# A Hymba decoder layer on one core: where the gates of the second in-projection stand, and which pages the first steps of the second out-projection use

## The chip, the cores and the metric

One Trainium2 chip, one of its cores. The metric is the device time of one execution in microseconds (us); of several runs the median is taken. TensorE (PE) multiplies; VectorE (DVE), ScalarE (ACT) and GpSimd (POOL) work element by element; SP issues most of the DMAs, POOL some of them.

## The reference

A single layer (depth 1) over 2048 positions of width 1024, all in float32, and a last RMSNorm. Without its input generator:

```python
h = rms_norm(x, norm1_g)
z = einsum('bsd,de->bse', h, w_in)              # 1024 -> 3584
lru_x, lru_gate, sc_b, sc_c, sc_x = split(z)    # 1024, 1024, 512, 512, 512
lru_x = causal_dwconv(lru_x, lru_conv_w) + lru_conv_b        # 4 taps
r = sigmoid(lru_x @ wa + ba); i = sigmoid(lru_x @ wx + bx)   # 16 heads of 64
a = exp(-8 r softplus(-lambda)); b = sqrt(1 - a^2) * i * lru_x
h_t = a_t h_(t-1) + b_t                                      # scan over positions
y_lru = h * gelu(lru_gate)
y_sc = sc_b * causal_dwconv(sc_c * sc_x, sc_conv_w)          # 3 taps
x = x + concat(y_lru, y_sc) @ w_out                          # 1536 -> 1024
h = rms_norm(x, norm2_g)
u = causal_dwconv(h @ w_up, ffn_conv_w)                      # 1024 -> 6144, 3 taps
x = x + (gelu(gate) * up) @ w_down                           # 3072 -> 1024
out = rms_norm(x, final_g)
```

## The kernel before, in words

**Halves and stages.** The positions are worked in two halves of 1024. In order of time: the first half's in-projection (`in_phase(0)`, to about 335 us), its out-projection (`sweeps(0, .., "o")`, to 455 us), the second half's in-projection (`in_blocks`, to 753 us), its out-projection (`sweeps(1, .., "o")`, to 886 us), then `up_phase(0)`, `sweeps(0, .., "d")`, `up_phase(1)` and `sweeps(1, .., "d")`, the feed-forward network of each half. Features lie on the 128 partitions, positions along the free axis.

**A product in three.** An operand in float32 is written as hi + lo by `split` (L229): ACT copies it to the faster matmul type (hi, L230), DVE subtracts that copy from it (lo, L231). A product is then hi by hi, hi by lo and lo by hi. So each weight or activation page that PE reads has first cost one ACT and one DVE instruction, 128x1024 or 128x512.

**Seven products for eight.** Most projections use a Strassen-like scheme: of a matrix and an operand cut in 2x2 blocks, seven block products are formed of blocks and of sums of blocks. A product in `in_blocks` is 4 k-slices of 3 matmuls 128x128 by 128x512, 12 matmuls.

**The second in-projection.** `in_blocks` goes through 14 pairs of output blocks: L0 B0 L1 X0 L2 X1 L3 L4 L5 B2 L6 X2 L7 X3. An L pair holds the LRU input and the LRU gate of 128 channels; B and X pairs belong to the short convolution. A loop turn j issues the first products of pair j between the last ones of pair j-1: first (W11), second (W12) of pair j, seventh (W22) of pair j-1, the gates, fourth (S2) of pair j, sixth (S4) of pair j-1, third (S1) and fifth (S3) of pair j. When pair j-1 is done, `finish` issues the convolution of its LRU input (`conv`, L345 on ACT and three taps L347 on DVE, into a page named cv), and in the next turn come its gates: `lru_gates` (8 small matmuls, L371) and `lru_scan`: eight sigmoids of 64x512 on ACT (L382), then, with table loads between them, exp, tanh, square, square root and gelu on ACT (L387 to L398) and on DVE L385, L390, L392, the scan over positions L395 and the product L400. The outputs are combined for the out-projection's seven operands by DVE (L553 to L560) and stored to DRAM by POOL (L217).

Each product's partial result is copied from PSUM by ACT (L679) or added by DVE (L683); a matmul into the same bank must wait for its copy.

**The second out-projection.** `sweeps` makes 7 sweeps of 3 steps, one sweep for each of the seven products; a step multiplies two k-slices of weight by two of activation for four row blocks, 24 matmuls (L995). For a step SP loads a weight page and an activation page raw (L1008), and `split` makes of them four pages: wh, wl, fh, fl. The activation pages are what POOL stored in the stage before. Step 3, the first of sweep 1, reads the operand T1, which the last two units end.

**Pages.** SBUF has a few rotating pools: 28 pages "act" (`act`; in `in_blocks` they hold the normed input of the half, and come free as the last pairs use it), 10 pages for split weights and for `in_blocks`' cv, r and output pages (`wpage`, `vpage`: whoever asks next gets the page that has been out longest), 6 raw pages, 7 temporaries, 2 + 2 big ones. Steps below `lead` put their four split pages in act pages, with priority LW; the others in wpages with priority HW:

```python
with tc.high_priority(offset=LW if step < lead else HW):
    ...
    home = act if step < lead or ... else wpage
```

**What sets the order.** PE, SP and POOL issue in program order. DVE and ACT are ordered by the compiler's scheduler, from dependencies and the priorities given by `high_priority`; once set, each engine runs its list in that order. So a change of program text on PE also moves DVE and ACT rows.

**Beside the sweeps.** During the second out-projection, `h_beside(0, ...)` prepares the up-projection's four operands of the first half (`h_prep`: two loads ha and hb, DVE L609 to L616, and four splits), one at each of the four named steps. `up_phase` starts with the split weights of its first two pairs (`up_weights`), a `spread` that does pair 0 k by k, and 23 further pairs. Before everything, PE runs `WARM` matmuls of ones (L1043), until the first operands are there.

Of the kernel before, what the change touches and what calls it, by code (L numbers as in the profile page):

```python
# [28 lines left out]
NR = 6  # L29
LP = 0  # L30
LW = 400
NS = 2
J0 = 2
LEAD = 3
HALVES = (slice(0, P // 2), slice(P // 2, P))
HW = 90
HE = 30
WARM = 9
NOUT = NLRU + NSC
NI = NFF // 2  # L40
NO = NOUT // 2
# [49 lines left out]
def block_kernel(  # L91
# [59 lines left out]
    def wpage(name):  # L151
        turn[0] += 1
        return wv_page(name, "w" if turn[0] * NW % NWV < NW else "v")
# [10 lines left out]
    def raw_tile(name):  # L164
        return page(name, "wr", NR)
# [462 lines left out]
    def up_weights(half, j):  # L628
        n = f"up{half}_{j}"
        ta, tb, tcd = (raw_tile(f"wr{k}_{n}") for k in "abc")  # L630
        nc.sync.dma_start(ta[:, 0, :], w_up[j, 0])
        nc.sync.dma_start(tcd, w_up[j, 2:4].rearrange("h p c -> p h c"))
        nc.sync.dma_start(tb[:, 0, :], w_up[j, 1])
        tick()

        def two(src, name):
            hi, lo = wpage(f"wh{name}_{n}"), wpage(f"wl{name}_{n}")
            split(hi, lo, src)
            return [(hi[:, i, :], lo[:, i, :]) for i in range(2)]

        def add(dst, a, b):
            nc.vector.tensor_tensor(dst, a, b, ALU.add)

        w11, w12, w22, w21 = ta[:, 0, :], tb[:, 0, :], tcd[:, 0, :], tcd[:, 1, :]
        s1, s2, s3, s4 = ta[:, 1, :], tb[:, 1, :], tcd[:, 1, :], ta[:, 1, :]
        add(s1, w22, w21)
        add(s2, s1, w11)
        add(s3, w11, w21)
        p11, p1 = two(ta, "a")
        p12, p2 = two(tb, "b")  # L650
        p22, p3 = two(tcd, "c")
        add(s4, s2, w12)
        d = wpage(f"whd_{n}")
        split(d[:, 0, :], d[:, 1, :], s4)
        return {"W11": p11, "W12": p12, "W22": p22, "S1": p1, "S2": p2, "S3": p3, "S4": (d[:, 0, :], d[:, 1, :])}
# [124 lines left out]
            combine_odd(f_d[half], when, j // 2, a, cu, c, (cg[:, :NB], cg[:, NB:]))  # L780

    def up_phase(half, hs, between):
        wts = [up_weights(half, 0), up_weights(half, 1)]
        cur = UpPair(half, 0, hs, wts[0])
        for j in range(NFF):
            if j + 2 < NFF:
                wts.append(up_weights(half, j + 2))
            nxt = UpPair(half, j + 1, hs, wts[j + 1]) if j + 1 < NFF else None
            if j == 0:
                cur.spread()  # L790
                nxt.begin()
                nxt.sum1()
            elif nxt is None:
                cur.middle(cur.sum1)
                cur.second()
                cur.fourth()
                cur.end()
            else:
                cur.middle(cur.second)
                nxt.begin()  # L800
                cur.fourth()
                if j + 2 < NFF:
                    nxt.sum1()
                cur.end()
            up_rest(half, j, cur.ug, cur.un)
            cur = nxt
            between(j)
# [76 lines left out]
    def in_blocks(hs, start):  # L884
        half = 1
        gates = {}
        gain = {}
        wts = [{} for _ in PAIRS]
# [46 lines left out]
        open_gates = []  # L935
        for j in range(count + 1):
            tick()
            load(*uses(j + 1), rest=j + 1 >= count)
            if j == 0:
                pairs[0].spread()  # L940
                finish(pairs[0])
                start(0)
                continue
            cur = pairs[j] if j < count else None
            prev = pairs[j - 1] if j > 1 else None
            if cur:
                cur.first_term()
                cur.second_term()
            if prev:
                prev.seventh_term()  # L950
            for name in open_gates:
                gated, scanned = gates.pop(name)
                scanned(gated())
            open_gates = []
            if cur:
                cur.fourth_term()
            if prev:
                prev.sixth_term()
                finish(prev)
            open_gates = list(gates)  # L960
            if cur:
                cur.third_term()
                cur.fifth_term()
            if j < count:
                start(j)
# [10 lines left out]
    def sweeps(half, wsrc, fsrc, ni, name, residual, done, beside, tail=0, lead=0):  # L976
# [6 lines left out]
        for s, (wo, fo, on_x) in enumerate(SWEEPS):  # L983
# [20 lines left out]
            for i2 in range(ni // 2):  # L1004
# [5 lines left out]
                parts = []  # L1010
                with tc.high_priority(offset=LW if step < lead else HW):
                    for raw, n in zip(raws, "wf"):
# [28 lines left out]
    warm = pst("warm")  # L1041
    for i in range(WARM):
        nc.tensor.matmul(warm[:, :P], ones, ones, start=True, stop=True)  # L1043
# [124 lines left out]
    def h_beside(half, at):  # L1168
        def beside(s):
            if s in at:  # L1170
                hs[half].append(h_prep(half, len(hs[half]), rs2[half][0]))

        return beside

    prepare = h_beside(0, (4, 8, 12, 17))

    def out1_beside(s):
        if s == 0:
# [13 lines left out]
        out1_beside,  # L1192
        lead=LEAD,
    )
# [4 lines left out]
    def beside_pairs(j):  # L1199
        mean1(j)  # L1200
        for _ in range(NS if j >= J0 else 0):
            sum_step()
# [156 lines left out]
```

## Time and profile before

| What | Value |
|---|---|
| median of 3 runs | 2275.21 us (2275.09 to 2276.2) |
| the profiled execution | 2275.72 us, its span 2273.9 us |
| PE busy | 2228.6 us, 98% of the span |
| DVE, ACT, POOL busy | 1788.1, 1214.4, 173.8 us |
| mean granted TensorE clock | 0.993 |

Times below are microseconds from the span's start. A row of the timeline gives the start, the duration, the engine, the line, the operation with its output and inputs, the shape, and in brackets the time for which the engine stood idle ahead of it and what it then waited for. PE's duration of one matmul (0.39 us) overlaps the next one's: from start to start it is 0.227 us at the full clock, so that 12 matmuls take 2.72 us. A row of the windows view gives, for a stretch, the busy time of each engine with its instructions, the granted clock as a share of the full one, the share of DMA time and the rate.

### The profile page before, as it was taken

The page shows a single profiled execution, that of the slowest core. Times are in us where ns is not written, and L with a number is a line of the kernel's source. Part 1 is how long each engine was busy: PE and PEld are TensorE (multiplying, and loading weights), DVE is VectorE, ACT ScalarE, POOL GpSimd, SP SyncE. Part 2 cuts the span into 40 slices and gives each one's busy share as a digit, 9 for nine tenths or more (in the row PEclk, how much of TensorE's full clock was granted, in tenths as well). Part 3 has the DMA queues.
Part 4 walks back from the last instruction along what each step waited for, and adds up shares of the span by engine and source line. Part 5 has one row for each costly group of instructions (what it writes and reads, how often), then busy time and mean ns, then how long its engine had stood idle before and what let it go on. Part 6 is the DMA issues. An engine that isn't in the chain of part 4 may idle for free.

```text
span 2273.9 us, 26402 instructions
## 1 busy us (share of the span) xinstructions
PE 2228.6 (98%) x9750; PEld 1819.8 (80%) x9750; DVE 1788.1 (79%) x2070; ACT 1214.4 (53%) x1403; POOL 173.8 (8%) x298
## 2 busy tenths in 40 slices
PE   9999999999989799999999999999999999999997
PEld 7787787888768588888888888888888888888886
DVE  8868878947777898898888887676988888876556
ACT  7648834457797544455554444454544444443343
POOL 0021110000000100012111100000000000000000
PEclk9999999999999899999999999999999999999999
DMA  7585367833533865488782357674233232359764
GB/s 280 158 235 173 111 235 246 296 112 130 172 116 110 288 242 205 149 219 252 206 203 99 117 188 284 216 258 152 84 103 116 91 118 88 118 189 347 245 196 155
DMA packets 157952, 415.00 MB, mean 183 GB/s; under 512 B 16640, under 2 KB 19328, under 8 KB 157248
## 3 DMA queue, kind: packets, MB, share of 16 engines
q1 hardware_dynamic: 136960, 356.96, 45.7%
q0 software_dynamic: 20720, 56.37, 9.5%
q8 instruction: 76, 1.25, 0.2%
q14 instruction: 52, 0.43, 0.1%
q10 hardware_dynamic: 144, 0.00, 0.0%
HBM read 311.55 MB, written 139.46 MB: 198 GB/s over the span
## 4 chain that ended last, share of the span: by engine, by line
PE 86%; DVE 5%; ACT 4%; issue 3%; DMA 1%; POOL 0%; DVEq 0%; SPq 0%; ACTq 0%; POOLq 0%
PE zx L668 22%; PE dx L995 11%; PE zc L668 11%; PE zin_b L286 10%; PE dy L995 9%; PE za L668 6%; PE ox L995 5%; PE oy L995 4%; PE zxin L668 3%; PE zcin L668 1%; PE zS L668 1%; PE zain L668 1%; PE zr_b L371 1%; PE zW L668 1%; DVE r L395 1%
## 5 line engine op out<-in xcount | busy, mean ns | idle before, releaser
L231 DVE TENSOR_TENSOR fl_d<-wrf_d,fh_d 128x1024 fp32r<-128x1024 f32 x84 | 102.6, 1223 | 121.4 <-ACT fh_d L230 119.0
L230 ACT ACTIVATE fh_d<-wrf_d 128x1024 fp32r<-128x1024 f32 x84 | 88.9, 1059 | 202.4 <-PE dy L995 77.8
L995 PE MATMUL dx<-fh_d,wl_d 128*128 128x512 f32 x384 | 149.4, 389 | 0.0
L995 PE MATMUL dx<-fl_d,wh_d 128*128 128x512 f32 x384 | 149.4, 389 | 0.0
L995 PE MATMUL dx<-fh_d,wh_d 128*128 128x512 f32 x384 | 149.4, 389 | 0.0
L286 PE MATMUL zin_b<-xh,wl_in 128*128 128x512 f32 x448 | 138.2, 389 | 2.6 <-DVE wl_in L231 2.6
L286 PE MATMUL zin_b<-xh,wh_in 128*128 128x512 f32 x448 | 139.3, 392 | 0.9 <-ACT wh_in L230 0.8
L286 PE MATMUL zin_b<-xl,wh_in 128*128 128x512 f32 x448 | 138.3, 390 | 0.1
L231 DVE TENSOR_TENSOR wla_up<-wra_up,wha_up 128x1024 fp32r<-128x1024 f32 x48 | 58.8, 1225 | 101.0 <-ACT wha_up L230 101.0
L347 DVE SCALAR_TENSOR_TENSOR cg<-ug,prm,cg 128x1024 f32<-128x1024 f32 x96 | 122.9, 1280 | 9.5 <-ACT cg L343 8.5
L347 DVE SCALAR_TENSOR_TENSOR cu<-un,prm,cu 128x1024 f32<-128x1024 f32 x96 | 122.7, 1278 | 4.6 <-ACT cu L343 4.3
L668 PE MATMUL zc<-hhB,whd_up 128*128 128x512 f32 x368 | 120.8, 389 | 0.0
L668 PE MATMUL zx<-ht,whc_up 128*128 128x512 f32 x368 | 113.3, 389 | 0.0
L995 PE MATMUL dy<-fh_d,wh_d 128*128 128x512 f32 x288 | 112.1, 389 | 0.0
L995 PE MATMUL dy<-fl_d,wh_d 128*128 128x512 f32 x288 | 112.1, 389 | 0.0
L995 PE MATMUL dy<-fh_d,wl_d 128*128 128x512 f32 x288 | 112.1, 389 | 0.0
L231 DVE TENSOR_TENSOR wl_d<-wrw_d,wh_d 128x1024 fp32r<-128x1024 f32 x84 | 102.2, 1218 | 8.6 <-ACT wh_d L230 7.2
L679 ACT ACTIVATE ug<-zx 128x512 f32<-128x512 f32 x92 | 54.8, 595 | 101.2 <-PE zx L668 96.4
L230 ACT ACTIVATE fh_o<-wrf_o 128x1024 fp32r<-128x1024 f32 x42 | 44.5, 1059 | 111.5 <-PE ox L995 36.7
L286 PEld LDWEIGHTS zin_b<-xh,wh_in 128*128 128x128 f32 x448 | 83.5, 188 | 24.4 <-DVE xl L422 3.0
L286 PEld LDWEIGHTS zin_b<-xh,wl_in 128*128 128x128 f32 x448 | 84.0, 188 | 20.4 <-DVE wl_in L231 3.0
L286 PEld LDWEIGHTS zin_b<-xl,wh_in 128*128 128x128 f32 x448 | 84.1, 188 | 18.0 <-DVE xl L455 0.6
(549 smaller groups left out, 6394.6 us busy)
## 6 DMA issues: line engine op xcount, KB each, us to landing
wrc_up<-in_w_up SPq DMA_DIRECT2D x48, 512.0 KB, 4.9
f_d_T<-cg SPq DMA_DIRECT2D x96, 256.0 KB, 2.5
wrw_d<-sd_d_S SPq DMA_DIRECT2D x48, 512.0 KB, 5.1
wrf_d<-f_d_T SPq DMA_DIRECT2D x48, 512.0 KB, 4.3
f_d_B<-cu SPq DMA_DIRECT2D x72, 256.0 KB, 2.5
wrw_d<-in_w_down SPq DMA_DIRECT2D x36, 512.0 KB, 4.8
wrf_d<-f_d_B SPq DMA_DIRECT2D x36, 512.0 KB, 3.3
wr_in<-in_w_in SPq DMA_DIRECT2D x25, 512.0 KB, 7.1
```

What stands on the lines that cost most here:

```text
L230: nc.scalar.activation(r32(hi), src, AF.Copy)
L231: nc.vector.tensor_tensor(r32(lo), src, hi, ALU.subtract)
L286: nc.tensor.matmul(ps[t], r32(a), r32(b[:, blk(t)]), start=(first and i == 0), stop=(last and i == 2))
L347: nc.vector.scalar_tensor_tensor(dst, src[:, k : k + T], col(o_w + k), dst, ALU.mult, ALU.add)
L371: nc.tensor.matmul(ps[t], gw[rows, :], cv[rows, blk(t)], start=True, stop=True)
L395: nc.vector.tensor_tensor_scan(h, a, i, init, ALU.mult, ALU.add)
L668: nc.tensor.matmul(ps, r32(p[:, s]), r32(self.hs[k][x][o]), start=f and i == 0, stop=l and i == 2, skip_group_check=True,)
L679: nc.scalar.activation(dst, self.x, AF.Copy)
L995: nc.tensor.matmul(ps[m], r32(p), r32(x[:, k, :]), start=first and i == 0 and n == 0, stop=(last or not on_x) and i == ni - 1 and n == 2, ...
```

## The change

There are five edits. The gates of an open L pair come, on PE, after the fourth product of pair j and not ahead of it (GP = 1; in the last turn, where there is no pair j, nothing moves). Five leading steps of the second out-projection and not three use act pages and priority LW. In both up phases, the first pair's `up_weights` is under a priority of its own (UPP), which the scheduler of DVE and ACT sees. There are eleven warm-up matmuls and not nine. And the four operands of the first up phase are prepared at steps 4, 10, 15 and 19 and not at 4, 8, 12 and 17.

```diff
-LEAD = 3
+LEAD = 5
+GP = 1
+UPP = 200
-WARM = 9
+WARM = 11
     def up_phase(half, hs, between):
-        wts = [up_weights(half, 0), up_weights(half, 1)]
+        with tc.high_priority(offset=UPP):
+            wts = [up_weights(half, 0)]
+        wts.append(up_weights(half, 1))
...
             if prev:
                 prev.seventh_term()
-            for name in open_gates:
-                gated, scanned = gates.pop(name)
-                scanned(gated())
-            open_gates = []
-            if cur:
-                cur.fourth_term()
+            for p in range(3):
+                if p == GP:
+                    for name in open_gates:
+                        gated, scanned = gates.pop(name)
+                        scanned(gated())
+                    open_gates = []
+                if p == 0 and cur:
+                    cur.fourth_term()
+                if p == 1 and prev:
+                    prev.sixth_term()
             if prev:
-                prev.sixth_term()
                 finish(prev)
...
-    prepare = h_beside(0, (4, 8, 12, 17))
+    prepare = h_beside(0, (4, 10, 15, 19))
```

The line numbers of the changed kernel are 2 higher than those before, 4 higher behind `up_phase`, 7 higher behind `in_blocks`. On PE and POOL nothing else moves; on SP the loads of the second to fourth of the operands move with their steps. DVE's and ACT's lists change from the second in-projection on.

The first place is DVE in turn 9 of `in_blocks`, ahead of the gates of L4 (cv_4 is the page that these gates read; r_3, i_3 belong to L3's scan; wS, wW are weights of pairs 9 and 10). Before:

```order
L390 SCALAR_TENSOR_TENSOR cv_3_4781<-r_3_4905,cv_3_4781 128x1024
L347 SCALAR_TENSOR_TENSOR cv_4_4960<-xlin_4712,prm,cv_4_4960 128x1024
L683 TENSOR_TENSOR soin_4990<-zcin_4965,soin_4990 128x512
L231 TENSOR_TENSOR wS_in_4848<-wr_in9S_9S_4845,wS_in_4848 128x512
L347 SCALAR_TENSOR_TENSOR cv_4_4960<-xlin_4712,prm,cv_4_4960 128x1024
L392 TENSOR_TENSOR i_3_4906<-i_3_4906,cv_3_4781 128x1024
L231 TENSOR_TENSOR wS_in_4851<-wr_in9S_9S_4845,wS_in_4851 128x512
L683 TENSOR_TENSOR sbin_5024<-zain_5039,sbin_5024 128x512
L395 SCALAR_TENSOR_TENSOR r_3_4905<-a_3_4907,h_last,i_3_4906 128x1024
L347 SCALAR_TENSOR_TENSOR cv_4_4960<-xlin_4712,prm,cv_4_4960 128x1024
```

and changed:

```order
L349 SCALAR_TENSOR_TENSOR cv_4_4962<-xlin_4714,prm,cv_4_4962 128x1024
L685 TENSOR_TENSOR soin_4992<-zcin_4967,soin_4992 128x512
L233 TENSOR_TENSOR wS_in_4850<-wr_in9S_9S_4847,wS_in_4850 128x512
L392 SCALAR_TENSOR_TENSOR cv_3_4783<-r_3_4920,cv_3_4783 128x1024
L233 TENSOR_TENSOR wS_in_4853<-wr_in9S_9S_4847,wS_in_4853 128x512
L349 SCALAR_TENSOR_TENSOR cv_4_4962<-xlin_4714,prm,cv_4_4962 128x1024
L685 TENSOR_TENSOR sbin_5026<-zain_5041,sbin_5026 128x512
L349 SCALAR_TENSOR_TENSOR cv_4_4962<-xlin_4714,prm,cv_4_4962 128x1024
L394 TENSOR_TENSOR i_3_4921<-i_3_4921,cv_3_4783 128x1024
```

The third tap of cv_4 has moved from behind L3's scan to ahead of the instruction that feeds it.

The second place is ACT in the turn ahead, around the eight sigmoids of L3 (L382 before, L384 changed) and the copy of L5's fourth product out of PSUM (xlin_4854, changed xlin_4856). The last two sigmoids and what followed, before:

```order
L382 ACTIVATE r_3_4905<-zi_3_b_4900,prm 64x512
L382 ACTIVATE i_3_4906<-zi_3_b_4900,prm 64x512
L679 ACTIVATE xlin_4854<-zxin_4856 128x512
L230 ACTIVATE wW_in_4833<-wr_in9W_8W_4827 128x512
L387 ACT_TABLE_LOAD
```

and the rows up to the first two sigmoids, changed:

```order
L681 ACTIVATE soin_4813<-zxin_4716 128x512
L400 ACTIVATE soin_4813<-soin_4813 128x1024
L232 ACTIVATE wW_in_4832<-wr_in9W_8W_4829 128x512
L681 ACTIVATE xlin_4856<-zxin_4858 128x512
L232 ACTIVATE wW_in_4835<-wr_in9W_8W_4829 128x512
L384 ACT_TABLE_LOAD
L384 ACTIVATE r_3_4920<-zr_3_b_4912,prm 64x512
L384 ACTIVATE i_3_4921<-zr_3_b_4912,prm 64x512
```

The copy of the fourth product's bank (xlin_4856) no longer stands behind the eight sigmoids, and the gelu of the unit before (L400) has come ahead of them.

The third place is DVE at the start of sweep 1 of the second out-projection (o_1_0 is step 3, o_1_1 step 4; soin_5649 and its like are the last unit's outputs, yc what is stored for T1 and its like, xr the residual). Before:

```order
L231 TENSOR_TENSOR wl_o_1_0_5969<-wrw_o_1_0_5964,wh_o_1_0_5968 128x1024
L392 TENSOR_TENSOR i_7_5785<-i_7_5785,cv_7_5730 128x1024
L560 SCALAR_TENSOR_TENSOR yc_10_5620<-yc_10_5620,soin_5155 128x512
L395 SCALAR_TENSOR_TENSOR r_7_5784<-a_7_5786,h_last,i_7_5785 128x1024
L1032 TENSOR_TENSOR xr_11_1_5930<-xr_11_1_5930,ox_2_5842 128x512
L400 TENSOR_TENSOR soin_5649<-soin_5649,r_7_5784 128x1024
L1032 TENSOR_TENSOR xr_11_0_5892<-xr_11_0_5892,ox_1_5841 128x512
L558 TENSOR_TENSOR soin_5327<-soin_5649,soin_5327 128x512
L559 SCALAR_TENSOR_TENSOR yc_8_5584<-yc_8_5584,soin_5649 128x512
L231 TENSOR_TENSOR fl_o_1_0_5973<-wrf_o_1_0_5966,fh_o_1_0_5972 128x1024
```

and changed (up to fl of step 4):

```order
L392 SCALAR_TENSOR_TENSOR cv_7_5732<-r_7_5786,cv_7_5732 128x1024
L233 TENSOR_TENSOR wl_o_1_0_5971<-wrw_o_1_0_5966,wh_o_1_0_5970 128x1024
L233 TENSOR_TENSOR fl_o_1_0_5975<-wrf_o_1_0_5968,fh_o_1_0_5974 128x1024
L925 SCALAR_TENSOR_TENSOR soin_5157<-soin_5762,soin_5157 128x512 x2
L394 TENSOR_TENSOR i_7_5787<-i_7_5787,cv_7_5732 128x1024
L560 TENSOR_TENSOR sbin_5026<-soin_5157,sbin_5026 128x512
L397 SCALAR_TENSOR_TENSOR r_7_5786<-a_7_5788,h_last,i_7_5787 128x1024
L561 SCALAR_TENSOR_TENSOR yc_10_5622<-yc_10_5622,soin_5157 128x512
L402 TENSOR_TENSOR soin_5651<-soin_5651,r_7_5786 128x1024
L562 SCALAR_TENSOR_TENSOR yc_10_5622<-yc_10_5622,soin_5157 128x512
L233 TENSOR_TENSOR wl_o_1_1_6011<-wrw_o_1_1_6006,wh_o_1_1_6010 128x1024
L560 TENSOR_TENSOR soin_5329<-soin_5651,soin_5329 128x512
L233 TENSOR_TENSOR fl_o_1_1_6015<-wrf_o_1_1_6008,fh_o_1_1_6014 128x1024
```

Both lo splits of step 3 have moved from behind the scan of the last unit (and what follows from it) to right behind L390, now L392; those of step 4 stand two and four rows behind that unit's product with its gate, L402.

## The prediction

> **What bounds the kernel now.** I read the waits of PE first, since PE is busy for 98% of the span; then its timeline around the longest of them; then DVE's, ACT's and POOL's timelines for what these waits wait for. PE's waits summed by what ended them, the lines that bear on the two projections of the second half:
>
> ```profile
> PE oy L995 <- DVE fl_o L231: 8.5, 3, 5.6
> PE zr_b L371 <- DVE cv L347: 8.1, 3, 5.7
> PE oy L995 <- ACT fh_o L230: 5.1, 2, 3.1
> ...
> PE zxin L668 <- ACT xlin L679: 1.3, 2, 0.9
> ```
>
> The columns are microseconds in total, times, the longest. They come to 23 us. From 905 us on PE is busy throughout, while DVE is free for a fifth of that stretch. Windows give the stretch, the busy time of PE, PE's weight loads, DVE, ACT and POOL (with instructions), then the granted clock, the DMA share and GB/s:
>
> ```profile
> 765.78:887.02 121.24, 108.56 (x457) 88.25 (x456) 113.84 (x130) 55.44 (x58) 5.60 (x12) 0.93 0.69 242
> 769.60:804.00 34.40, 21.72 (x73) 16.51 (x73) 29.73 (x32) 10.47 (x12) 5.40 (x10) 0.75 0.73 242
> 804.00:885.60 81.60, 81.60 (x361) 67.57 (x360) 78.91 (x89) 40.55 (x42) 0.20 (x2) 1.00 0.69 246
> 905.00:2259.00 1354.00, 1354.00 (x5976) 1121.20 (x5975) 1069.83 (x1188) 651.97 (x742) 99.76 (x166) 1.00 0.54 175
> ```
>
> So what the change can win lies in two places: A, the gates in the second in-projection, and B, steps 3 to 5 of the second out-projection, where PE is busy 21.72 of 34.40 us at a clock of 0.75.
>
> Place A. Gates of L4, then of L5, on PE; and the DVE and ACT rows around them:
>
> ```profile
> 629.34 0.50 PE L668 MATMUL zxin<-hhB11x,wS_in 128*128 128x512 f32 x1 [0.92 <-ACT xlin L679]
> 637.64 2.88 PE L668 MATMUL zxin<-htx,wW_in 128*128 128x512 f32 x12
> ...
> 642.54 2.34 DVE L395 TENSOR_TENSOR_SCAN r<-a,h_last,i 128x1024 f32<-128x1024 f32 x1
> 644.80 1.26 DVE L347 SCALAR_TENSOR_TENSOR cv<-xlin,prm,cv 128x1024 f32<-128x1024 f32 x1
> 646.21 1.19 PE L371 MATMUL zr_b<-cv,gw 64*128 64x512 f32 x1 [5.69 <-DVE cv L347]
> 648.29 0.68 ACT L382 ACTIVATE r<-zr_b,prm 64x512 f32<-64x512 f32 x1 [0.27 <-PE zi_b L371]
> 649.63 0.50 PE L668 MATMUL zxin<-hhT1x,wS_in 128*128 128x512 f32 x1
> 661.72 0.57 ACT L679 ACTIVATE soin<-zxin 128x512 f32<-128x512 f32 x1
> 670.85 0.67 PE L371 MATMUL zr_b<-cv,gw 64*128 64x512 f32 x1 [1.86 <-DVE cv L347]
> 672.77 0.50 PE L668 MATMUL zxin<-hhT1x,wS_in 128*128 128x512 f32 x1
> ```
>
> PE has finished the seventh product at 640.36 (637.64 + 2.72) and stands until cv's third tap is done, because DVE runs L3's scan ahead of that tap. The gates then take 646.21 to 649.63, 3.42 us, where L5's take 1.92 (670.85 to 672.77): half clock.
>
> Place B. Sweep 0 ends at 769.66. The first matmuls that waited in steps 3 and 4, step 6's first one, and what DVE, ACT and POOL did:
>
> ```profile
> 772.94 0.80 PE L995 MATMUL oy<-fh_o,wh_o 128*128 128x512 f32 x1 [3.12 <-ACT fh_o L230]
> 779.37 0.80 PE L995 MATMUL oy<-fl_o,wh_o 128*128 128x512 f32 x1 [5.63 <-DVE fl_o L231]
> 788.24 0.50 PE L995 MATMUL oy<-fh_o,wh_o 128*128 128x512 f32 x1 [1.95 <-ACT fh_o L230]
> 790.72 0.80 PE L995 MATMUL oy<-fl_o,wh_o 128*128 128x512 f32 x1 [1.98 <-DVE fl_o L231]
> 804.01 0.39 PE L995 MATMUL ox<-fh_o,wh_o 128*128 128x512 f32 x1
> ```
>
> ```profile
> 765.78 1.22 DVE L390 SCALAR_TENSOR_TENSOR cv<-r,cv 128x1024 f32<-128x1024 f32 x1
> 766.92 1.29 DVE L921 SCALAR_TENSOR_TENSOR soin<-soin,soin 128x512 f32<-128x512 f32 x2
> ...
> 772.32 2.35 DVE L395 TENSOR_TENSOR_SCAN r<-a,h_last,i 128x1024 f32<-128x1024 f32 x1
> 778.10 1.22 DVE L231 TENSOR_TENSOR fl_o<-wrf_o,fh_o 128x1024 fp32r<-128x1024 f32 x1
> 771.84 1.06 ACT L230 ACTIVATE fh_o<-wrf_o 128x1024 fp32r<-128x1024 f32 x1 [2.21 <-DVE i L392]
> 787.13 1.06 ACT L230 ACTIVATE fh_o<-wrf_o 128x1024 fp32r<-128x1024 f32 x1 [14.24 <-DMA y_d_B<-soin]
> 778.59 0.55 POOL L217 DMA_DIRECT2D y_d_T<-yc  x1 [37.27 <-DVE yc L559]
> ```
>
> Three steps of 24 matmuls at 0.227 us end 16.3 us after 769.66, at 785.98; step 6 starts at 804.01. So 18.0 us are lost, 12.7 as waits (3.12 + 5.63 + 1.95 + 1.98), the rest as half clock. Step 3 waits for a page (L392 frees it) and then for its lo split, which DVE does behind the scan; step 4's fh waits for a page that the POOL stores hold.
>
> **The change part by part. A, gates later.** The fourth product, 12 matmuls or 2.72 us, now covers part of the wait, and the third tap stands ahead of the scan (2.26 us) and of L392. I walk the new lists with the trace's pitches (128x1024: 1.14 to 1.2 on DVE, 1.06 on ACT; 512 wide: 0.6 and 0.53). L4's fourth-bank copy wait of 629.34 (start to start 1.08) goes, since that copy now precedes the sigmoids: PE ends the fourth product at 640.36 - 1.08 + 2.72 = 642.0. L3's sigmoids start some 1.7 us later than now, because a gelu and copies have come ahead of them; with them the square (638.0), L392 in its new numbering (639.5) and then a split, a tap, an add and the third tap: cv is there at about 643.3. Wait 1.3; gates end at 645.2.
>
> Then ACT: L4's sigmoids start at about 648.2, as now. The copy that the next seventh product needs ended 14.0 us behind that start (648.29 to 662.29), so again at 662.1, while PE, five products behind its gates, arrives at 645.2 + 13.6 = 658.8: a **new wait of 3.2**. Then seventh and fourth product (5.4, 667.5) and L5's gates without a wait: 669.5. Now the same work ends at 672.77 + 2.72 = 675.5. Gain 6.0. If the sigmoids run right behind the gates there is no such wait, 7.6 at most; if a table load in that list waits for a page as well, some 2.3 more is lost, 3.7 at least.
>
> To it come small waits on other turns (0.41 and 0.40, about 1.1 from start to start; the first of them on a weight split):
>
> ```profile
> 568.89 0.73 PE L668 MATMUL zxin<-hhB11x,wW_in 128*128 128x512 f32 x2 [0.41 <-DVE wW_in L231]
> 598.77 0.50 PE L668 MATMUL zxin<-hhT1x,wS_in 128*128 128x512 f32 x1 [0.40 <-ACT xlin L679]
> ```
>
> I take them as gone (0 to 1.1). Against it: the sigmoids of every L pair now start 2.7 us later for PE, so the copy for the seventh product, which had some 3 us to spare, has 0.3 to 1; I charge 0.9 for all of them (0 to 3, a third of a microsecond a pair and up). A stand of 3.2 us can be followed by half clock; the gates of L4 paid 3.42 - 1.92 = 1.5. Charged whole (0 to 1.5). Sum of A: -6.0 - 1.1 + 0.9 + 1.5 = **-4.7** (-8.7 to +0.8).
>
> The granted clock decides that 1.5. An idle time of 2.58 us at 371.69 was followed within 1.4 us by matmuls of 0.63, one of 2.59 at 104.28 by matmuls of 0.39:
>
> ```profile
> 371.69 0.50 PE L995 MATMUL ox<-fl_o,wh_o 128*128 128x512 f32 x1 [2.58 <-DVE fl_o L231]
> 373.07 0.63 PE L995 MATMUL ox<-fh_o,wh_o 128*128 128x512 f32 x1
> ...
> 104.28 0.73 PE L286 MATMUL zin_b<-xh,wl_in 128*128 128x512 f32 x2 [2.59 <-DVE wl_in L231]
> 104.86 0.39 PE L286 MATMUL zin_b<-xh,wh_in 128*128 128x512 f32 x1
> ```
>
> [...]
>
> **B, five leading steps.** Steps 3 and 4 get act pages, free since the last pairs used them, so fh no longer waits for L392 or the stores. Their splits come earlier in DVE's list: L390's end at 766.92, wl 768.05, fl **769.2** (two times 1.14), before PE needs it: step 3 loses nothing. Then the two halves of L921 (1.3), L392 (1.1), 0.6, the scan (2.26), 0.6, L400 (1.1), 0.6, wl of step 4 (1.1), 0.6 and fl (1.1): **779.8**. Step 3 ends at 775.1 and step 4's second matmul comes 0.2 later: a wait of **4.4**, and 1.7 of half clock behind it (the 18.0 less the 12.7 leave 5.3 for three stands). The work that was done late because of the early splits, the outputs of the last units, reaches POOL 2.25 us later than the first store now (778.59). Step 5 has its pages in time; step 6's pages hang on the stores: 0.9. Then 7.0 of the 18.0 stay: **-11.0**.
>
> DVE has one gap just behind the sweep:
>
> ```profile
> 901.29 1.22 DVE L231 TENSOR_TENSOR wlb_up<-wrb_up,whb_up 128x1024 fp32r<-128x1024 f32 x1 [6.94 <-PE zS L668]
> ```
>
> From both sides: if the last unit's ACT and DVE work were not in the way at all, DVE itself ends it, with 113.84 of 121.24 us busy; 7.4 idle, and 4.6 of splits move behind the sweep into the idle 6.94 ahead of 901.29, so at most 12. If step 6 stood as step 4 did at 788.24 (1.95) with another 1.7 of half clock, and not 0.9, 2.8 more would be lost: 8.2. I take 8 to 12, and the walk's 11.
>
> **The rest.** Operands at 10, 15, 19: the same DVE work, later, among steps that have 81.60 us with no wait; the fourth is needed in the spread 14 us behind the sweep. UPP moves the first up weights, late in the sweep, ahead of neighbours. Both 0; without cover, each 128x1024 split that came late would cost 1.2. Warm-ups:
>
> ```profile
> 1.00 3.77 PE L1043 MATMUL warm<-ones 128*128 128x128 f32 x18 [1.00 <-POOL eps L119]
> 5.56 1.12 PE L286 MATMUL zin_b<-xh,wh_in 128*128 128x512 f32 x2 [0.79 <-ACT wh_in L230]
> ```
>
> 18 records in 3.77 us are 0.21 each; two warm-ups, four records, 0.84, end at 5.6, where PE would have waited: 0 (to 0.1).
>
> Sum: -4.7 - 11.0 = -15.7 on the profiled execution of 2275.72, half a microsecond above the median: **2260.0**. The half microsecond is less than the runs' own spread (1.1), and is left.
>
> **The rivals.** The first rests on this window:
>
> ```profile
> 618.00:652.40 34.40, 27.80 (x113) 19.86 (x113) 23.40 (x27) 33.19 (x43) 2.70 (x5) 0.95 0.34 107
> ```
>
> *ACT is late at every L pair, and step 4 longer.* The 0.3 to 1 us that the copies have to spare is used up: 1 us at each of the six other L pairs eats A (-4.7 - 0.9 + 6 = 0.4), and B comes to its lower bound of 8: 2267 to 2269. For it: ACT is busy 33.19 of 34.40 us in 618.00 to 652.40. Against: the copies of the fourth products now precede the sigmoids, where 628 to 629 shows one that did not. Chance 0.17.
>
> *More than forecast.* No new wait at the seventh product and no half clock (A near -8), B at its bound of 12: -20, 2255.7. Chance 0.08.
>
> *It doesn't do what it says at A.* The wait for cv turns whole into the wait for the copy on ACT: A 0, B -11: 2264.7. Inside the range. For it: the 14.0 us from the sigmoids to that copy have not become shorter. Against: the walk, in which five products cover most of them. Chance 0.13.
>
> *Slower.* Eight fewer calls for split pages, four at each of two steps, shift which of the ten rotating pages each later weight split gets, all through both up phases. If a pair's weights then get a page that its predecessor's matmuls still read, PE stands once a pair; from 0.34 us at each of 46 pairs the whole 15.7 is gone, at 0.45 the time is 2280. For it: these lists do differ in both up phases. Against: no wait of PE in 1354 us, and DVE free for 284 of them. Chance 0.04.
>
> **How the numbers follow.** The forecast, 2257 to 2264, has 0.54; with the third rival, whose time lies beside it, 0.67. Unlisted small mishaps (a late load at a moved step) have 0.04 and lie near no change. The range takes in the forecast, most of the ACT rival and half of the larger gain: 2255 to 2268.5. A change below 0.2%, 4.5 us, can't be told from none. Faster: 0.54 + 0.17 + 0.08 + 0.13 = 0.92. Same 0.04, slower 0.04.
>
> **What would show it.** Right: PE's first matmul of L4's gates waits under 2 us for cv and one on zxin about 3 for soin; step 3 has no wait, step 4 one of about 4.4 on fl_o; step 6 begins near 788 (804.0 less 4.7 and 11); PE has no wait in the up phases. Wrong: waits on soin or xlin in most turns; waits of fh_o on stores in step 4 or 5; a wait on wlb_up or its like in the up phases.

## The result, and the profile after

| | before | changed |
|---|---|---|
| median of 9 runs, us | 2277.05 | 2270.40 |
| ratio | | 0.9972 (0.9962 to 0.9982) |
| profiled execution and its span, us | 2275.72, 2273.9 | 2269.55, 2267.7 |

The kernel became faster by 0.28%, 6.4 us, where 15.7 were forecast; 2270.4 lies outside the range of 2255 to 2268.5.

PE is busy nearly all the time in both kernels, so the span can be cut at PE's first matmul of each stage. The windows view of the kernel before, with the second in-projection (from the matmul behind its spread), the second out-projection and the first up phase:

```profile
473.83:753.34 279.51, 268.80 (x1162) 210.94 (x1160) 200.84 (x244) 215.53 (x285) 17.24 (x32) 0.99 0.41 134
753.34:885.61 132.27, 119.59 (x505) 97.41 (x504) 120.24 (x133) 67.03 (x70) 5.60 (x12) 0.94 0.73 257
885.61:1343.48 457.87, 457.87 (x2022) 379.14 (x2020) 385.23 (x438) 233.86 (x275) 62.74 (x117) 1.00 0.60 174
```

and of the changed one:

```profile
475.48:757.21 281.73, 271.67 (x1162) 212.82 (x1160) 201.06 (x244) 214.98 (x286) 17.23 (x32) 0.98 0.40 134
757.21:878.01 120.80, 116.52 (x505) 95.48 (x504) 114.82 (x128) 64.20 (x67) 5.40 (x10) 0.99 0.77 281
878.01:1337.47 459.46, 458.34 (x2022) 379.03 (x2021) 389.54 (x443) 236.14 (x278) 63.27 (x119) 1.00 0.59 173
```

The first figure behind each stretch is its length. Place B paid as forecast: 120.80 for 132.27, -11.5 (forecast -11.0). Place A cost 2.2 where it was to gain 4.7. The first up phase, forecast unchanged, is 1.6 longer. The in-projection also starts 1.65 later (475.48 for 473.83), of which more below; what follows the first up phase differs by 0.2 in all. Sum: 1.65 + 2.2 - 11.5 + 1.6 - 0.2 = -6.2, the difference of the spans.

PE's waits of the changed kernel, summed by what ended them (total, times, longest):

```profile
PE zxin L670 <- ACT soin L681: 4.7, 2, 2.7
PE oy L1002 <- DVE fl_o L233: 4.5, 2, 3.6
...
PE zxin L670 <- ACT wW_in L232: 3.2, 1, 3.2
...
PE zx L670 <- ACT ug L681: 1.1, 1, 1.1
PE zr_b L373 <- DVE cv L349: 1.1, 1, 1.1
```

The waits of 8.1 on cv are down to one of 1.1 in the last turn, and those for fh_o are gone. New are a wait for a weight split on ACT (wW_in), which no step of the prediction had; a second and longer wait for copies named soin (one of 0.9 before), which it had in turn 10; and one in the up phase (ug).

The second in-projection by turns, from PE's first matmul of a turn to that of the next (turn 9 holds the gates of L4, turn 10 those of L5; two of the experiments stand beside):

| turn | before | changed | gates late only for L3, L4, L5 | all but L2's late |
|---|---|---|---|---|
| 6 | 22.19 | 22.30 | 22.49 | 23.41 |
| 7 | 19.75 | 22.65 | 19.71 | 19.72 |
| 8 | 22.40 | 24.49 | 21.18 | 21.18 |
| 9 | 28.47 | 21.34 | 23.31 | 22.90 |
| 10 | 23.11 | 25.58 | 25.73 | 25.54 |

(The third kernel is the one called pages_turned below.) Turns 9 and 10, which the walk was about, gained 4.7. Turns 7 and 8 lost 5.0, and the last two turns 1.65 (two waits, for a copy and for cv, that were 1.1 and 0.55 shorter before).

The stand that opens turn 8, in the timeline of the changed kernel:

```profile
605.30 2.35 DVE L397 TENSOR_TENSOR_SCAN r<-a,h_last,i 128x1024 f32<-128x1024 f32 x1
...
608.15 1.22 DVE L402 TENSOR_TENSOR soin<-soin,r 128x1024 f32<-128x1024 f32 x1
...
611.09 0.69 DVE L685 TENSOR_TENSOR xlin<-zcin,xlin 128x512 f32<-128x512 f32 x1
611.81 1.24 ACT L347 ACTIVATE cv<-xlin,prm 128x1024 f32<-128x1024 f32 x1 [6.14 <-DVE xlin L685]
613.90 1.14 ACT L232 ACTIVATE wW_in<-wr_in8W_8W 128x512 fp32r<-128x512 f32 x2
614.57 0.79 PE L670 MATMUL zxin<-hhB11x,wW_in 128*128 128x512 f32 x1 [3.15 <-ACT wW_in L232]
616.16 1.22 PE L670 MATMUL zxin<-hhB11x,wW_in 128*128 128x512 f32 x2 [0.37 <-DVE wW_in L233]
```

Read it from the end. PE waits 3.15 us for a weight split on ACT. ACT is not busy: it has stood for 6.14 us ahead of the row in front, the convolution of L3, which needs the last add into xlin. That add runs on DVE at 611.09, behind the scan of L2 (605.30) and five rows on the units' outputs. Before, L2's scan started at 600.41 (602.06, with the 1.65 of the later start), and the split of a first weight stood ahead of the convolution:

```profile
603.28 0.62 ACT L230 ACTIVATE wW_in<-wr_in8W_8W 128x512 fp32r<-128x512 f32 x1
608.24 1.24 ACT L345 ACTIVATE cv<-xlin,prm 128x1024 f32<-128x1024 f32 x1 [4.33 <-DVE xlin L683]
609.38 0.62 ACT L230 ACTIVATE wW_in<-wr_in8W_8W 128x512 fp32r<-128x512 f32 x1
```

ACT stood here too, 4.33 us, but PE had its first weights. Behind the new stand the clock is halved for 6.8 us (0.51, the figure behind POOL's):

```profile
613.70:620.60 6.90, 5.66 (x13) 3.99 (x14) 6.87 (x9) 2.86 (x6) 0.54 (x1) 0.51 0.73 249
```

### The profile page after: what moved, and what is told of

It is laid out like the page before. It is cut to its first block, busy times and chain, and to the rows that moved or that the text cites. A ratio compares the mean times of both kernels' runs of the same rounds, so it can differ in the third digit from the quotient of the medians.

```text
span 2267.7 us, 26408 instructions
## 1 busy us (share of the span) xinstructions
PE 2231.3 (98%) x9754; PEld 1821.9 (80%) x9754; DVE 1787.3 (79%) x2070; ACT 1212.4 (53%) x1403; POOL 174.4 (8%) x298
## 4 chain that ended last, share of the span: by engine, by line
PE 87%; DVE 5%; issue 3%; ACT 3%; DMA 2%; SPq 0%; POOL 0%; DVEq 0%; ACTq 0%; POOLq 0%
PE zx L670 22%; PE dx L1002 12%; PE zc L670 11%; PE zin_b L288 10%; PE dy L1002 9%; PE za L670 5%; PE zxin L670 5%; PE ox L1002 4%; PE oy L1002 3%; PE zcin L670 2%; PE zain L670 1%; PE zS L670 1%; PE zr_b L373 1%; PE zW L670 1%; ACT r L384 0%
```

## The experiments

All times were taken beside runs of the kernel before on the same chip (medians 2277.14, 2276.49 and 2276.88 in the three groups); ratios are to these. The stage times are of one profiled execution each.

### Place A: which pair's gates cost

**The changed kernel again**, nothing edited.

> The changed kernel once more, nothing edited, for a second profile. Two theories of where the gain of the later gates went. Lists: ACT's new order in turn 7 (the convolution's ACT row of L3 ahead of pair 8's weight split) and in the last turns gives it back. Then the wait of 3.2 us on the weight split, the wait of 2.7 on the seventh product of turn 9 and that of 1.1 in the first up phase are there again, and the second in-projection takes 281 to 282 us again; the half-clock stretches may lie elsewhere. Clock: the loss is half clock that fell so by chance; then the stretch comes out 3 us or more shorter or longer.

0.9972 (0.9962 to 0.9981), 2270.56. The in-projection took 281.19, the out-projection 121.64, the up phase 460.05, with the same waits at the same places. So the stands are set by the lists, not by chance.

**Gates back.**

```diff
-GP = 1
+GP = 0
```

> The changed kernel with the gates ahead of the fourth product again (GP = 0), all else changed. Lists: the second in-projection takes as long as before (279.5), the waits on the weight split in turn 7 and on soin in turn 13 are gone, the wait of 5.7 on cv is back; against the changed kernel 2 us faster, against the kernel before 9 to 12 faster, ratio 0.9955. By the prediction's own sum it would be 4.7 slower than the changed kernel, ratio near 0.999.

0.9966 (0.9952 to 0.9979), 2269.69: the change without its first edit is as fast as the whole, 7.5 us below the kernel before where 9 to 12 were expected. In-projection 279.29, as before (279.51); out-projection 120.94. The up phase took 463.05, with a wait of 3.1 on ug: that loss needs no late gates.

**Gates late for L3, L4 and L5 only.**

```diff
-                if p == GP:
+                if p == (GP if j in (8, 9, 10) else 0):
```

> The changed kernel with the gates behind the fourth product in turns 8, 9 and 10 alone, where L3's, L4's and L5's gates stand, and ahead of it in all others. Lists: turns 7 and 13 are as before, L4 and L5 keep their 6 us, so the second in-projection takes 273 to 275 and the time is 8 us below the changed kernel's, some 2261, ratio 0.993. If late gates as such are to blame (each L pair's sigmoids start 2.7 us later and ACT hands the lateness on), the wait comes up in turns 10 to 12 and the time is near the changed kernel's or above.

0.9957 (0.9945 to 0.9970), 2265.87. In-projection 277.37, not the 273 to 275 expected: the wait for the seventh product's copy was followed by half clock (a clock of 0.68 from 661.50 to 668.50). The stand at turn 8 is gone. But the up phase took 463.24; its wait has grown:

```profile
1113.66 0.69 DVE L644 TENSOR_TENSOR wra_up<-wrc_up 128x512 f32<-128x512 f32 x1 [4.88 <-DMA wrc_up<-in_w_up]
1114.27 0.68 DVE L685 TENSOR_TENSOR ug<-zc,ug 128x512 f32<-128x512 f32 x1
...
1117.62 0.50 PE L670 MATMUL zx<-hhB,whc_up 128*128 128x512 f32 x1 [3.33 <-ACT ug L681]
```

A sum of up weights, which waits 4.88 us for a load, stands on DVE ahead of the add that PE's next bank needs.

**All gates late but L2's.**

```diff
-                if p == GP:
+                if p == (0 if j == 6 else GP):
```

> The changed kernel with one turn undone: in turn 6 (L2's gates) they stand ahead of the fourth product again. Lists: L2's late gates put L2's scan and what follows it ahead of the add that L3's convolution waits for, and so ACT's row of it ahead of pair 8's weight split; without them the wait of 3.2 us on that split and the one of 0.4 behind it go, with their half clock: the second in-projection takes 274 to 276, 6 to 7 less than the changed kernel's 281.5. If lateness gathers over the turns, turn 6 alone gives a seventh of it, a microsecond.

0.9955 (0.9941 to 0.9969), 2267.16; in-projection 278.15, where 274 to 276 were expected. One pair's gates put back, and the stand at turn 8 is gone (turn 7: 19.72). That settles its cause. The weight split stands ahead of the convolution again, and L4's gates now wait 1.13, where the prediction had 1.3 and the changed kernel nothing:

```profile
604.96 0.62 ACT L232 ACTIVATE wW_in<-wr_in8W_8W 128x512 fp32r<-128x512 f32 x1
609.92 1.24 ACT L347 ACTIVATE cv<-xlin,prm 128x1024 f32<-128x1024 f32 x1 [4.34 <-DVE xlin L685]
645.32 0.66 PE L373 MATMUL zr_b<-cv,gw 64*128 64x512 f32 x1 [1.13 <-DVE cv L349]
```

So the stand at turn 8 had covered that wait: while PE stood, ACT and DVE caught up. By the table of turns, the stand costs turns 7 and 8 some 6.2 us (47.14 against 40.89 with the third kernel's lists) and gives 2.0 of them back in turn 9. With L0's, L1's and L6's gates late too, turn 6 and the last turns cost more than the smaller edit's, so 278.15 is not the best.

**The gates alone**, in the kernel before.

```diff
+GP = 1
...
+            for p in range(3):
+                if p == GP:
+                    for name in open_gates:
...
```

> The kernel before with the later gates alone. By the prediction's sum the second in-projection takes 274.8 (279.5 less 4.7) and the time falls by as much, ratio 0.998. By the lists it takes 281 to 282 as in the changed kernel, the second out-projection stays at 132, and the first up phase has a wait of its own, since its list too has the add behind the load: ratio 1.000 to 1.003.

1.0001 (0.9992 to 1.0010), 2277.28. In-projection 282.96, with the same wait of 3.1 for wW_in; out-projection 131.33. The first up phase took 459.49, with a wait of 1.3 for a copy (un). No page call is missing here, and DVE has the add on ug (1125.07) ahead of the sum of up weights (1129.81) as before; but that sum waits 4.06 us for its load. So a wait of a microsecond there can come without shifted pages. Place A as written is worth nothing, whichever kernel it is put into.

### The up phase: pages

**Gates late for L3, L4, L5, and the page counter turned on** by the eight calls that steps 3 and 4 no longer make.

```diff
+    turn[0] += 8
     sums(w_down, sd_d, NI)
```

> Late gates in turns 8, 9 and 10 alone, and the page counter turned on by eight behind the second out-projection, so that the up phases ask the two groups of rotating pages in the order they had before. Pages: the wait of ug's copy in the first up phase (1.5 to 4.3 us from start to start in the runs so far, with or without half clock behind it) comes of the eight page calls that five leading steps don't make; with them counted it is gone, the first up phase takes 458 and the time falls by 4 to 6, to some 2261. Arrival: the wait comes of a weight load that lands late because that phase starts 10 us earlier; then it stays.

0.9940 (0.9927 to 0.9952), **2262.58**, the best of all. Its three stages by the windows view:

```profile
475.67:751.72 276.05, 269.16 (x1162) 211.41 (x1160) 200.65 (x244) 215.43 (x286) 17.25 (x32) 0.99 0.41 136
751.72:872.49 120.77, 116.50 (x506) 95.39 (x505) 114.52 (x127) 65.44 (x69) 5.57 (x12) 0.99 0.78 281
872.49:1330.51 458.02, 458.02 (x2022) 379.06 (x2021) 390.04 (x444) 235.04 (x277) 63.61 (x117) 1.00 0.60 174
```

The wait in the up phase is gone, and DVE's rows there stand in the old order again, the add first:

```profile
1107.58 0.68 DVE L685 TENSOR_TENSOR ug<-zc,ug 128x512 f32<-128x512 f32 x1
1109.58 0.69 DVE L644 TENSOR_TENSOR wra_up<-wrc_up 128x512 f32<-128x512 f32 x1 [1.32 <-DMA wrc_up<-in_w_up]
```

So the wait on ug came from the eight missing calls for pages. That is the trigger of the prediction's slower rival, but not its mechanism: no weight page is shown to be still in use; DVE's list has another order, and it costs something at one pair and not at 46.

**The same, and the squares of the first half a turn earlier**, so that ACT and DVE have them out of the way of turn 10.

```diff
-    mean0 = squares_then_mean(..., "b0", rs2[0], 1)
+    mean0 = squares_then_mean(..., "b0", rs2[0], 0)
```

> As the kernel before it in this list, and the eight squares of the first half's residual one turn earlier each (turns 1 to 8 and not 2 to 9), so that turn 9's ACT list has one instruction of 1.04 us less between L3's square root and L4's sigmoids. If the wait of some 2.7 us on the copy for the seventh product in turn 10 is ACT's list, run row behind row, it shrinks by about 1, to 1.7, and the half clock behind it (6.8 us of it in the last run) may go: 1 to 4.5 us faster. If it comes of what the list waits for (a page, a DVE result), it stays.

0.9948 (0.9934 to 0.9962), 2264.77: no gain. The wait for the seventh product's copy shrank to 1.8. But the first square now stands in turn 0, and a copy is late there:

```profile
483.70 0.79 PE L670 MATMUL zxin<-hhT1x,wS_in 128*128 128x512 f32 x1 [2.38 <-ACT sbin L681]
```

In-projection 278.22, 2.2 longer. The wait moved.

### Place B: what carries the 11.5

**Five leading steps alone**, in the kernel before.

```diff
-LEAD = 3
+LEAD = 5
```

> The kernel before with five leading steps and nothing else. If the leading steps carry the gain of 11.5 in the second out-projection alone, its 132.3 us become 121 to 122, ratio 0.995. If the operands' later steps (10, 15, 19) are needed for it, because DVE has 7 us to spare in that stretch, a part of the gain is missing: 125 or more. The wait of 1.1 in the first up phase is there if the shifted page calls make it, and not if the priority of the first up weights or the operands' steps do.

1.0009 (1.0001 to 1.0018), 2278.61: if anything slower. Out-projection 130.47, a gain of 1.8. Steps 3 and 4 did what was forecast, but step 9 now waits, and 10.2 us of half clock follow (a clock of 0.66 from 812.00 to 827.00). The first up phase took 464.70, with a wait of 4.0 on ug: five leading steps alone bring that wait. SP's issues, DVE, ACT and PE ahead of step 9:

```profile
793.50 0.32 SPq L1008 DMA_DIRECT2D wrf_o<-y_d_T  x1
805.76 1.22 DVE L231 TENSOR_TENSOR hlB<-ha,hhB 128x1024 fp32r<-128x1024 f32 x1
807.04 0.32 SPq L603 DMA_DIRECT2D ha<-x_d  x1
808.14 0.32 SPq L603 DMA_DIRECT2D hb<-x_d  x1
808.51 0.42 SPq L1008 DMA_DIRECT2D wrw_o<-in_w_out  x1
814.55 1.06 ACT L230 ACTIVATE wh_o<-wrw_o 128x1024 fp32r<-128x1024 f32 x1 [8.04 <-DMA wrw_o<-in_w_out]
816.94 0.79 PE L995 MATMUL oy<-fh_o,wh_o 128*128 128x512 f32 x1 [4.74 <-ACT fh_o L230]
```

SP issues nothing for 13 us. Then the loads of the second operand go out, ha 0.06 us after DVE's split of the first operand's ha ends (806.98), and only behind them the weights of step 9. So by the times the loads wait for the first operand's pages, and the weights stand in the queue behind loads. Before, DVE came to that split 11 us earlier:

```profile
794.59 1.21 DVE L231 TENSOR_TENSOR hlB<-ha,hhB 128x1024 fp32r<-128x1024 f32 x1
795.87 0.32 SPq L603 DMA_DIRECT2D ha<-x_d  x1
```

and the same load followed it just as closely. With five leading steps the splits of steps 6 to 8 have come ahead of it on DVE (fl of step 6 from 794.53, the last one from 802.22).

**The later operand steps alone.**

```diff
-    prepare = h_beside(0, (4, 8, 12, 17))
+    prepare = h_beside(0, (4, 10, 15, 19))
```

> The kernel before with the operands at steps 10, 15 and 19 and nothing else. If the later operands only relieve DVE once PE is ahead, steps 3 and 4 wait as before (12.7 us) and the second out-projection takes 131 to 133: ratio 0.999 to 1.001. If they carry the gain by themselves, it takes 125 or less.

1.0016 (1.0007 to 1.0024), 2280.12: slower. Out-projection 133.33, and the up phase 460.87 with waits for first up weights (wlb_up 1.1, whd_up 0.5).

**Both together.**

> The kernel before with five leading steps and the operands at steps 10, 15 and 19; gates, priority and warm-ups as before. If these two edits together carry the gain of 11.5 in the second out-projection, it takes 121 to 122 and step 9 does not wait; the time is 11 less a wait in the first up phase of 4 to 6: ratio 0.997. If the priority of the first up weights has a share, the stretch is longer than the changed kernel's by that share.

0.9993 (0.9985 to 1.0002), 2276.09, where 0.997 was expected. Out-projection 121.52: together they give 10.8, where apart they gave 1.8 and -1.1. But the up phase took 465.84, with the wait on ug (2.9) and a stand at its first product:

```profile
872.87 1.22 DVE L231 TENSOR_TENSOR hlT<-hc,hhT 128x1024 fp32r<-128x1024 f32 x1
874.01 2.47 DVE L1032 TENSOR_TENSOR xr<-xr,ox 128x512 f32<-128x512 f32 x4
...
877.00 1.22 DVE L231 TENSOR_TENSOR wla_up<-wra_up,wha_up 128x1024 fp32r<-128x1024 f32 x1
878.27 0.80 PE L668 MATMUL zW<-hhB,wla_up 128*128 128x512 f32 x1 [2.92 <-DVE wla_up L231]
```

The last operand's work, now at step 19, pushes the first up weight behind it.

**No priority for the first up weights**, in the best kernel.

```diff
-UPP = 200
+UPP = 0
```

> The fastest kernel so far (late gates in turns 8, 9 and 10, page counter turned on by eight) without the priority of the first up weights. The prediction gave that edit 0. If it is what keeps the first up weights ahead once the second out-projection ends 11 us earlier, PE waits some 3.3 us near the start of the first up phase, with or without half clock, as it did with the leading steps and the operands alone: 3 to 5 slower than with it, some 2266.

0.9975 (0.9966 to 0.9985), 2272.40. The out-projection is unchanged (120.78), the first up phase took 465.16 for 458.02, with the same stand of 3.92 for wla_up, and the second up phase 461.59 for 457.87. With the priority that split is done long before PE comes; in the changed kernel at

```profile
870.71 1.22 DVE L233 TENSOR_TENSOR wla_up<-wra_up,wha_up 128x1024 fp32r<-128x1024 f32 x1
```

So the priority, which the prediction had at 0, is worth some 8 to 10 us here (the ratios 0.9975 and 0.9940, the medians 9.8 apart), once the operands are late; 3 to 5 were expected.

**Nine warm-ups**, in the best kernel.

```diff
-WARM = 11
+WARM = 9
```

> The same fastest kernel with nine warm-ups. The first product's start hangs on ACT, 0.8 us behind the ninth: 0 to 0.2 of a difference, which this measurement can't tell from none.

0.9936 (0.9922 to 0.9951), 2262.83: no difference. PE's first product starts at 5.98 instead of 5.96; the two matmuls only fill a wait for wh_in. The first up phase took 459.32, with a wait of 1.2 for a weight split (wlc_up) near its start: a microsecond there comes and goes.

The second out-projection and the first up phase side by side, in us:

| leading steps | operand steps | priority | gates | out-projection | first up phase | ratio |
|---|---|---|---|---|---|---|
| 3 | old | no | old | 132.27 | 457.87 | 1 |
| 5 | old | no | old | 130.47 | 464.70 | 1.0009 |
| 3 | new | no | old | 133.33 | 460.87 | 1.0016 |
| 3 | old | no | all late | 131.33 | 459.49 | 1.0001 |
| 5 | new | no | old | 121.52 | 465.84 | 0.9993 |
| 5 | new | yes | old | 120.94 | 463.05 | 0.9966 |
| 5 | new | yes | all late | 120.80 | 459.46 | 0.9972 |
| 5 | new | yes | L3 to L5 late, pages turned | 120.77 | 458.02 | 0.9940 |
| 5 | new | no | L3 to L5 late, pages turned | 120.78 | 465.16 | 0.9975 |

## Why the prediction was wrong, point by point

**A, the walk of L4 and L5: right.** Forecast: a wait of 1.3 for cv, then a new one of 3.2 for the seventh product's copy, half clock behind it (1.5), net -4.5. Where nothing else is disturbed the cv wait was 1.1 and the copy's 2.7, and turns 8 to 10 gained 3.8 (70.22 for 73.98, the third kernel of the table) or 4.4 (69.62, the fourth). In the changed kernel:

```profile
668.70 1.65 PE L670 MATMUL zxin<-htx,wW_in 128*128 128x512 f32 x3 [2.70 <-ACT soin L681]
```

with a clock of 0.55 from 668.70 to 672.10, as charged.

**A, "I charge 0.9 for all of them": the step that failed.** The charge was for the copies of the other L pairs, which had 0.3 to 1 us to spare, bounded at 3. What cost most was no copy for the seventh product but a weight split, and at one pair: L2's late scan moved the last add into xlin, L3's convolution waited for it, and the split of pair 8's first weight stood behind that convolution on ACT. With the half clock that cost 5.0 in turns 7 and 8, and 1.65 more came in the last two turns: 0.55 on cv, and 1.1 on the copy for the last pair's seventh product. That copy had no "3 us to spare", for PE waited for it already; before and changed:

```profile
745.00 0.50 PE L668 MATMUL zxin<-htx,wW_in 128*128 128x512 f32 x1 [0.89 <-ACT soin L679]
```

```profile
748.29 0.50 PE L670 MATMUL zxin<-htx,wW_in 128*128 128x512 f32 x1 [1.99 <-ACT soin L681]
```

Together 6.6, against the 0.9. The walk had been made for one place, and the same edit acts at seven; at the others only the copies were looked at, though every row that waits on ACT or DVE ahead of a split is such a risk. The changed lists showed the convolution ahead of that split; I had not asked what it waits for.

**A, the small waits, -1.1: not gained.** The first, on a weight split, stayed and grew (0.68 for 0.41); the second went, and one of 0.37 came behind the stand at turn 8. Nothing is left of it in the table (turn 6: 22.30 for 22.19).

**B, -11.0: right in its sum (-11.5) and in its picture, wrong in what it ascribed it to.** Step 3 did not wait. Step 4 did, for fl_o, 3.6 where the walk had 4.4, and step 6 0.7 where it had 0.9:

```profile
782.98 0.50 PE L1002 MATMUL oy<-fl_o,wh_o 128*128 128x512 f32 x1 [3.62 <-DVE fl_o L233]
796.44 0.50 PE L1002 MATMUL ox<-fl_o,wh_o 128*128 128x512 f32 x1 [0.66 <-DVE fl_o L233]
```

But the leading steps alone give 1.8 of it: step 9 stands behind SP's loads for the operands unless these come later.

**"Both 0", for the operand steps and the priority: wrong apart, right in the sum.** The later operand steps bring 9.0 to the out-projection once there are five leading steps (130.47 to 121.52), and cost the up phase a stand, which the priority takes away. The prediction said that each 128x1024 split that came late would cost 1.2 without cover; one that came late cost 7.1 in the first up phase (465.16 for 458.02), since PE stands for all of the rows ahead of the split (3.92 us) and then runs at half clock (matmuls of 0.63 behind the stand, of 0.39 ahead of it). Two edits that apart gain nothing make, with a priority that was not run alone, one that gains 11.

**The up phases, 0: wrong by 1.6.** "No wait of PE in 1354 us" was true of the old lists. The slower rival's page shift happened, and its price was one stand of 1.1 us (1.7 when the kernel ran again). In the kernels with the gates back and with only three late, which also make eight calls fewer, it was 3.1 and 3.3 and cost 5.2 and 5.4. That the third kernel of the table has none, and that five leading steps alone bring one of 4.0, shows that the page count puts the sum ahead of the add; how long the stand is hangs on the sum's load. The gates alone, without the shift, had a stand of 1.3 at another copy and the same 1.6, so what the shift alone costs in the changed kernel is not shown. That rival, at 0.04 and priced at 46 pairs, had no smaller form, and a smaller form is what came.

**The start, +1.65: not the change**, but chance in the profiled execution. See the last section.

**The rivals.** "ACT late at every L pair, and step 4 longer", 2267 to 2269 at 0.17, came nearest in time, but neither of its two halves happened: ACT was late at one pair and in the last two turns, and step 4's wait was shorter than forecast. Of the 9.5 us between the forecast and the profiled execution (2269.55), A has 6.9, the up phase 1.6 and the start 1.65, less 0.5 from B and 0.2 elsewhere.

**What stays open.** Why the scheduler put L3's convolution ahead of that split when L2's gates were late. An edit that keeps all gates late and moves only that split was not run, nor were the priority alone and all gates late with the pages turned.

## What to carry to other kernels

When an edit acts at every pass of a loop, walk each pass and not only the one it was made for: ask of each row that stands ahead of an operand's split in its engine's list what it waits for (ACT stood 6.14 us ahead of one, with the split behind it), and how much later that now is. A group of edits that repair each other is not a sum of single prices; ask of each what the others make late, in each queue, the loads' too. And where a rotation of pages is shifted, put the count back or look for the one place in the later stages where a load-bound row has come ahead of one that TensorE needs.

## What the runs showed of the hardware

**A stand of one length can cost half clock or not; it hangs on where it falls.** From about 102 us PE waits for wl_in in every kernel, 2.6 us, with the same rows around it. In the profile of the changed kernel half clock followed and cost the 1.65 us, in that of the kernel before none did, with nothing changed ahead of it but two warm-ups: over 104.30 to 108.00 the clock was 0.61 and 1.00 (1.00 with the gates back, 0.57 in the best kernel). It followed in nine of the fourteen profiled executions of this study and not in the other five, of kernels with nine and with eleven warm-ups in either group; the best kernel had it with eleven and not with nine, the kernel before with nine not, but three edits of it with nine had.

The windows view shows what it went with. Within one execution half clock began only at moments that lie whole multiples of one length apart, 3.413 us, a third of the 10.24 for which it lasted before from 772.16 (0.50 over 772.16 to 782.40). Before it began at 372.80, 645.87, 772.16, 789.23 and 2263.79 (80, 37, 5 and 432 times 3.413 from one to the next), changed at 105.15, 374.80, 613.73, 668.35, 784.40 and 2258.96 (79, 70, 16, 34 and 432 times). Carried back from 372.80, this grid cuts the stand of the kernel before in two; in the changed kernel one window holds it all. Before, then changed:

```profile
99.74:103.15 3.41, 1.95 (x9) 1.30 (x7) 3.41 (x5) 1.06 (x1) 0.00 (x0) 1.00 1.04 367
103.15:106.56 3.41, 2.28 (x10) 1.90 (x11) 3.41 (x6) 1.06 (x1) 0.88 (x1) 1.00 1.10 400
```

```profile
101.74:105.15 3.41, 0.84 (x4) 0.71 (x5) 3.41 (x6) 1.79 (x2) 0.88 (x1) 1.00 0.93 368
105.15:108.56 3.41, 3.41 (x10) 2.64 (x9) 3.41 (x7) 1.28 (x2) 0.59 (x1) 0.50 1.12 416
```

PE was idle for 1.46 and 1.13 us of the two windows before, and for 2.57 of the one in the changed kernel, which is followed by half clock (0.50). At this stand the nine executions had 2.0 to 2.6 us of it in one window, the five 1.4 to 1.7 at most. Over the fourteen executions, from 15 to 2240 us, 63 of 64 full-clock windows with 1.9 us or more of idle PE were followed by half clock, and one of 114 with 0.6 to 1.9. In those of the kernel before and of the changed one alone it was nine of ten, and none of 16. An estimate from these counts: a stand below 1.9 us costs no half clock, one above 3.9 does, since half of it falls into one window, and in between it depends on where the stand falls.

**A half clock lasted 3.4 us or a multiple.** It lasted 3.41 us from 668.35 and 6.83 from 613.73 in the changed kernel, 10.24 from 772.16 before, and 10.24 from 814.38 with the leading steps alone, at waits of 2.7, 3.15, 3.12 and 4.7. Only the last one of an execution, before from 2263.79, goes on to the span's end (0.50 to 2273.90). Waits of 2.58 and 2.70 sufficed: the one ahead of 371.69 before (0.50 from 372.80 to 376.21) and the one ahead of 668.70 changed (0.50 from 668.35 to 671.76).

**A stand of PE is partly paid back.** The one at turn 8 cost 6.2 us and saved 2.0 in turn 9, as the engines that feed PE worked on in the meantime. So a wait that is removed can show one that it had hidden (1.13 for cv).
